# Second block of a two-block transformer: earlier norm sums, attention heads in pairs, one key chain, and low parts of weights moved from GpSimd to VectorE

## The chip, the cores and the metric

One core of one Trainium2 chip. The metric is the device time of one execution in microseconds (us). The kernel before took 2730.98 us (median of three runs, 2726.55 to 2734.91).

## The reference, cut to what matters

512 tokens, width 1024, two model blocks of two layers each, all in float32. The change touches the mixers of the second block only: the first layer adds retention (4 heads) and sliding-window attention (8 heads, 2 key/value heads), the second axial attention (8 heads, 2 key/value heads); each is followed by a feed-forward layer.

```python
def rms_norm_2(x, g):
    y = xf * lax.rsqrt(jnp.mean(xf * xf, axis=-1, keepdims=True) + EPS)
    return (y * g.astype(jnp.float32)).astype(x.dtype)
...
y = rms_norm_2(fwd + bwd, gn_gain.reshape(RET_HEADS, RET_DV))
return jax.nn.silu(g) * y
...
s = jnp.einsum('bqkgd,bjkd->bkgqj', qi, k, preferred_element_type=jnp.float32) * scale
p = jax.nn.softmax(s, axis=-1)
return jnp.einsum('bkgqj,bjkd->bqkgd', p.astype(v.dtype), v)
```

Queries and keys of both attentions pass an rms norm over the 128 numbers of a head; the window attention adds a bias and a sink to the softmax.

## The kernel before

Every product in float32 is made of three matmuls: each operand is split into a high part (`h`, `xh`) and a low part (`lo`, `xl`), and `mm3` (L413, L414, L415) adds high·high, low·high and high·low; such a group is called a triple below. Activations lie transposed, 128 of the 1024 features on the partitions and the 512 tokens along the row. `gemm` makes 128 output columns from a weight slab of 8 x 128 x 128 with 8 triples; `values` (L1031 to L1033) makes 256 columns for 128 tokens at a time with 32 triples of half the width, so it needs two slabs.

`fetch` brings each weight slab: a DMA into `w`, the high part on ScalarE (`h`, L394), the low part by a subtraction (`lo`, L395) on VectorE (DVE). For the last 24 slabs of the retention and window layer and the last 14 of the axial layer, `idle(i)` puts that subtraction on GpSimd (POOL).

A norm goes through three steps. TensorE (PE) adds the squares of a token by a product with ones (`tokens`, L481; for queries L1071). A chain of small DVE operations on 128 x 4 numbers (`rsqrt`, L492: a first guess and three Newton steps) makes the inverse root. `bcast` splits the result, multiplies it into an identity (`ssp`, two DVE operations), and PE spreads it over the partitions (L521), from where ScalarE copies it (L525).

`even` does retention by heads: query and key, two gate products, values, then the retention products; the norm of a head is finished by `head_end` in the next head's turn, with sums, chain and broadcast in one call ahead of the gates (the scheduler put the broadcast into the second gate). It then does the window attention, `attend` for one head at a time: scores (L1096 to L1098), softmax on DVE and ScalarE, transposes of the probabilities (L1125), product with the values (L1135 to L1137). Between a head's scores and its transposes comes the query product of the head after the next. `odd` does the same for axial attention, with the rotary products of a query on DVE and their sum on POOL (`rp`, L421). Keys have a chain of their own each (`kscale`).

Each engine works through its own queue in order. A scheduler writes these queues from the order of the calls and from priorities (`high_priority`). PSUM tiles have the tags `acc` (3 buffers), `s` (2), `tr` (2) and `o` (1).

Of the kernel before, what the change touches and what calls it, by code (L numbers as in the profile page):

```python
# [16 lines left out]
S = 512  # L17
# [282 lines left out]
def build(tc, a, upto=None):  # L300
# [74 lines left out]

    n_ffn = len(ffn_plan("w_mlp_up_2", "w_mlp_down_2", 1))
    odd1 = len(plan) - n_ffn
    even1 = odd1 - 20 - n_ffn
# [669 lines left out]
    def ksquare(mk, acc):  # L1048
        sq = Sum(own=mk("ksq"))
        sq.add(acc)  # L1050
        return sq

    def kscale(mk, sq, name):

        m = sq.tokens(P, 0.0)
        mul(m, m, rt[:, NB:])
        nc.vector.tensor_scalar_add(m, m, EPS)
        y = rsqrt(m)
        mul(y, y, rt[:, 0:NB])
        return bcast(y, out=mk(name))  # L1060

    def qsquare(mk, mkp, acc):
        f = mk("qsf")
        nc.scalar.activation(f, acc, AF.Square)
        return f

    def qstats(qs, i, sp):
        st_ps = ps("s")
        for b in range(NB):
            o = st_ps[:, 2 * b:2 * b + 1]  # L1070
            nc.tensor.matmul(o, sp[:, b * P:(b + 1) * P], onesf[:, 0:1], start=True, stop=True)  # L1071
        nc.vector.tensor_copy(qs[:, i], st_ps[:, 0:2 * NB].rearrange("p (b t) -> p b t", t=2)[:, :, 0])

    def qscale(qs):

        for i in range(2):
            stt(qs[:, i], qs[:, i], 1.0 / P, rt[:, NB:])
# [7 lines left out]
    def attend(mp, q, k, v, vcol, qs, bias, sink, oT, near):  # L1085
# [3 lines left out]
        lohi = [(max(0, b - 1) * P, min(NB, b + 2) * P) if near else (0, S) for b in range(NB)]  # L1089
        pt = []  # L1090
        for b in range(NB):
            lo, hi = lohi[b]
            n = hi - lo
            s = ps("s")
# [22 lines left out]
        yield  # L1117
        o = ps("o")
        order = (1, 0, 2, 3) if near else range(NB)
        for i, kb in enumerate(order):  # L1120
            b0, b1 = (max(0, kb - 1), min(NB, kb + 2)) if near else (0, NB)
            tr = ps("tr")
            for b in range(b0, b1):
                c = kb * P - lohi[b][0]
                nc.tensor.transpose(tr[:, b * P:(b + 1) * P], pt[b][:, c:c + P], ident)  # L1125
            pr = mp.tile([P, 2, S], F32R, name="pt", bufs=3)
            c0, c1 = b0 * P, b1 * P
            split(pr[:, 0, c0:c1], pr[:, 1, c0:c1], tr[:, c0:c1])
            f1 = c1
            if i == 0 and c1 < S:  # L1130
                nc.gpsimd.memset(pr[:, 0, c1:].bitcast(F32), 0.0)
                f1 = S
# [4 lines left out]
            nc.tensor.matmul(o[:, c0:c1], v1, pr[:, 0, c0:c1], start=False, stop=i == NB - 1)  # L1137
        split(oT[:, 0], oT[:, 1], o)

    def even(getr, xs, finish):  # L1140
# [6 lines left out]
        with contextlib.ExitStack() as st:  # L1147
# [5 lines left out]
            gacc = [gate(0, 0)]  # L1153
            y, later = getr()
            gacc.append(gate(0, 1))
# [5 lines left out]
            def head_end(h, sq, of, gs):  # L1161
                rr = bcast(rsqrt(sq.tokens(256)), out=mk("rr"), tag="s")
# [8 lines left out]
            for h in range(RH):  # L1171
# [42 lines left out]
                done = (h, sq, of, gs)  # L1214
            kacc = gemm2(*[slab(_gemm(e, 0, _rng(S_K + P * i))) for i in range(2)])
            head_end(*done)

        with contextlib.ExitStack() as st:
            mp = pool("sw", 1, st)
            mk = lambda name: mp.tile([P, S], F32, name=name, tag="p", bufs=NP)  # L1220
            mkp = lambda: mp.tile([P, 2, S], F32R, name="pt", bufs=3)
            ks = []
            sqk = [ksquare(mk, acc) for acc in kacc]
            vs = values(e, S_V, lambda: mp.tile([P, 2, 256], F32R, name="v", bufs=4))
            for i in range(2):
                m = kscale(mk, sqk[i], "km")
# [4 lines left out]
                ks.append(k)  # L1231

            qs, qq = {}, {}

            def query(h):

                g, i = divmod(h, 2)
                if h >= 8:
                    return
                if i == 0:  # L1240
                    qs[g] = mp.tile([P, 2, NB], F32, name="qs", bufs=3)
                acc = gemm(slab(_gemm(e, 0, _rng(S_Q + P * h))))
                q = mp.tile([P, 2, S], F32R, name="q", bufs=4)
                split(q[:, 0], q[:, 1], acc, vc("swa_q_norm_2"))
                qstats(qs[g], i, qsquare(mk, mkp, acc))
                qq[h] = q
                if i == 1:
                    qscale(qs[g])

            for h in range(2):  # L1250
                query(h)
            for h in range(SWH):
                g, i = divmod(h, 2)
                bias = mp.tile([P, 384], F32, name="bias", bufs=2)
                nc.sync.dma_start(bias, bias_view(h))
                oT = yo()
                at = attend(mp, qq[h], ks[h // 4], vs, P * (h // 4), qs[g][:, i], bias, vc("sink", h), oT, True)
                next(at)
                query(h + 2)
                list(at)  # L1260
                sw.append(oT)
                k0 = SWA_FILL[g]
                if i == 1 and k0 is not None:
                    outproj("w_out_even_2", k0, ys[k0:k0 + 4] if k0 < 8 else sw[0:4], xs)
# [4 lines left out]
    def odd(getr, xs, finish):  # L1269
# [6 lines left out]
        with contextlib.ExitStack() as st:  # L1276
            mp = pool("ax", 1, st)
            mk = lambda name: mp.tile([P, S], F32, name=name, tag="p", bufs=NP)
# [3 lines left out]
            tk = [mk("tk") for _ in range(2)]  # L1282
            for i in range(2):
                nc.vector.tensor_scalar_mul(tk[i], tab[:, i], vc("ax_k"))
            ks = []
            sqk = [ksquare(mk, acc) for acc in accs]
            fk = [rope(mk, acc, tk) for acc in accs]
            for i in range(2):
                nc.vector.tensor_scalar_mul(tab[:, i], tab[:, i], vc("ax_q"))
            vs = values(o, D + 256, lambda: mp.tile([P, 2, 256], F32R, name="v", bufs=4))  # L1290
            for i in range(2):
                m = kscale(mk, sqk[i], "km")
# [4 lines left out]
            oTs, qs, qq = [], {}, {}  # L1297

            def query(h):
                g, i = divmod(h, 2)  # L1300
                if h >= 8:
                    return
                if i == 0:
                    qs[g] = mp.tile([P, 2, NB], F32, name="qs", bufs=3)
                acc = gemm(slab(_gemm(o, 0, ax_cols(P * h))))
                f = rope(mk, acc, (tab[:, 0], tab[:, 1]))
                q = mp.tile([P, 2, S], F32R, name="q", bufs=4)
                split(q[:, 0], q[:, 1], f)
                qstats(qs[g], i, qsquare(mk, mkp, acc))
                qq[h] = q  # L1310
                if i == 1:
                    qscale(qs[g])

            for h in range(2):
                query(h)
            for h in range(8):
                g, i = divmod(h, 2)
                oT = op.tile([P, 2, S], F32R, name="yo", bufs=8)
                at = attend(mp, qq[h], ks[h // 4], vs, P * (h // 4), qs[g][:, i], None, None, oT, False)
                next(at)  # L1320
                if h >= 6:
                    outproj("w_out_odd_2", 0, oTs[0:4], xs, ns=(2 * i, 2 * i + 1))
                query(h + 2)
                list(at)
                oTs.append(oT)
# [106 lines left out]
    def getr2(sq=sq):  # L1432
        y1 = rsqrt(sq.tokens(D))
        r1 = small("tr%d" % NB)
        m = sg.tokens(D, 0.0)
        with tc.high_priority(offset=60):
            mul(r1, y1, y1)
            mul(m, m, r1)
            nc.vector.tensor_scalar_add(m, m, EPS)
            y = rsqrt(m)  # L1440
            mul(rt[:, 0:NB], y, y1)
            mul(rt[:, NB:], rt[:, 0:NB], rt[:, 0:NB])

        def later():
            r1b = bcast(y1, name="r2b")
# [104 lines left out]
```

## Time and profile before

| | us |
|---|---|
| median of three runs | 2730.98 |
| lowest, highest | 2726.55, 2734.91 |
| the profiled execution | 2728.14 |
| its span | 2726.4 |
| PE busy | 2675.7 (98%) |
| DVE busy | 2030.2 (74%) |
| ACT (ScalarE) busy | 1276.3 (47%) |
| POOL busy | 165.8 (6%) |

PE is busy nearly all the time, so what can be won is where PE waits, and what it does slowly. The mixers of the second block lie at about 1430 to 1830 us (retention, window attention) and 2190 to 2410 us (axial attention). The profile's share of busy time says little there: a wait of a few us at one place is read from the list of waits and from the timeline. The granted clock of 0.993 is a mean over the span; in short stretches it is far lower.

### The profile page before, as it was taken

How to read it: one execution, taken by the hardware profiler on the slowest of the kernel's cores; microseconds unless marked ns; L12 is line 12 of the kernel's file. 1: busy time of each engine (PE TensorE's matmuls, PEld its weight loads, DVE VectorE, ACT ScalarE, POOL GpSimd, SP SyncE). 2: the span in 40 equal slices, each digit the busy share in tenths (PEclk: the TensorE clock that was granted, in tenths of full speed). 3: DMA queues.
4: the chain of work that ended last, by engine and by line, in shares of the span. 5: the costliest groups of instructions: out<-in, count | busy, mean ns of one | idle time of the engine just before them, and what ended most of it. 6: DMA issues, size and time to landing. Idle time of an engine off the chain costs nothing.

```text
span 2726.4 us, 37828 instructions
## 1 busy us (share of the span) xinstructions
PE 2675.7 (98%) x14484; PEld 2279.0 (84%) x14484; DVE 2030.2 (74%) x3860; ACT 1276.3 (47%) x2071; POOL 165.8 (6%) x127
## 2 busy tenths in 40 slices
PE   8999999999999999999998999999999989999999
PEld 6887889999877778899987877888999877789998
DVE  8647778877775677988867656679878767798785
ACT  4437654433354674543443334565434436654442
POOL 0110000000000000000010012310000032100000
PEclk9999999999999999999999999999999999999999
DMA  4331423233434224333232221223233211123332
GB/s 162 104 112 55 140 85 124 93 97 98 136 102 157 78 74 143 105 105 101 94 107 71 86 71 61 79 73 101 96 107 109 93 62 39 55 100 101 103 107 70
DMA packets 80477, 262.83 MB, mean 96 GB/s; under 512 B 9223, under 2 KB 13063, under 8 KB 80296
## 3 DMA queue, kind: packets, MB, share of 16 engines
q1 hardware_dynamic: 80296, 260.41, 29.6%
q8 instruction: 114, 1.87, 0.3%
q14 instruction: 67, 0.55, 0.1%
HBM read 248.06 MB, written 12.32 MB: 96 GB/s over the span
## 4 chain that ended last, share of the span: by engine, by line
PE 90%; DVE 6%; ACT 1%; POOL 1%; issue 1%; DMA 0%; SPq 0%; POOLq 0%; DVEq 0%; ACTq 0%
PE ps_acc L415 18%; PE ps_acc L413 18%; PE ps_acc L414 18%; PE ps_tr L415 4%; PE ps_tr L413 4%; PE ps_tr L414 4%; PE ps_s L413 3%; PE ps_s L414 3%; PE ps_s L415 3%; PE ps_o L413 1%; PE ps_o L415 1%; PE ps_o L414 1%; PE ps_tr L956 1%; POOL rp L421 1%; PE ps_acc L1031 1%
## 5 line engine op out<-in xcount | busy, mean ns | idle before, releaser
L394 ACT ACTIVATE h<-w 128x1024 fp32r<-128x1024 f32 (+1 forms) x329 | 346.7, 1055 | 724.8 <-PE ps_acc L414 416.5
L414 PE MATMUL ps_acc<-y,h 128*128 128x512 f32 x1024 | 399.9, 391 | 0.0
L415 PE MATMUL ps_acc<-y,lo 128*128 128x512 f32 x1024 | 399.9, 390 | 0.0
L413 PE MATMUL ps_acc<-y,h 128*128 128x512 f32 x1024 | 399.8, 391 | 0.0
L395 DVE TENSOR_TENSOR lo<-w,h 128x1024 fp32r<-128x1024 f32 (+1 forms) x291 | 354.1, 1218 | 48.9 <-ACT h L394 48.2
L421 DVE TENSOR_TENSOR zg<-zg,ps_acc 128x512 f32<-128x512 f32 x304 | 207.6, 684 | 215.0 <-PE ps_acc L415 214.7
L413 PE MATMUL ps_acc<-xh,h 128*128 128x512 f32 x816 | 328.1, 402 | 0.0
L415 PE MATMUL ps_acc<-xh,lo 128*128 128x512 f32 x816 | 327.9, 402 | 0.0
L414 PE MATMUL ps_acc<-xl,h 128*128 128x512 f32 x816 | 326.4, 400 | 0.0
L415 PEld LDWEIGHTS ps_acc<-y,lo 128*128 128x128 f32 x1024 | 192.3, 188 | 40.8
L413 PEld LDWEIGHTS ps_acc<-y,h 128*128 128x128 f32 x1024 | 192.2, 188 | 37.1 <-ACT y L633 1.1
L414 PEld LDWEIGHTS ps_acc<-y,h 128*128 128x128 f32 x1024 | 192.3, 188 | 36.4 <-DVE y L634 0.8
L413 PE MATMUL ps_tr<-xh,h 128*128 128x256 f32 (+1 forms) x592 | 184.2, 311 | 8.0 <-ACT h L394 7.4
L415 PEld LDWEIGHTS ps_acc<-xh,lo 128*128 128x128 f32 x816 | 155.5, 191 | 34.7 <-issue 1.7
L413 PEld LDWEIGHTS ps_acc<-xh,h 128*128 128x128 f32 x816 | 155.5, 191 | 34.3 <-issue 2.3
L414 PEld LDWEIGHTS ps_acc<-xl,h 128*128 128x128 f32 x816 | 155.7, 191 | 33.9 <-issue 1.0
L415 PE MATMUL ps_tr<-xh,lo 128*128 128x256 f32 (+1 forms) x592 | 183.9, 311 | 0.0
L414 PE MATMUL ps_tr<-xl,h 128*128 128x256 f32 (+1 forms) x592 | 182.6, 309 | 0.0
L429 ACT ACTIVATE sh<-w 128x512 fp32r<-128x512 f32 x224 | 136.2, 622 | 59.6 <-PE ps_o L414 27.0
L430 DVE TENSOR_TENSOR sl<-w,sh 128x512 fp32r<-128x512 f32 x224 | 147.6, 682 | 0.0
L415 PE MATMUL ps_s<-th,sl 128*128 128x256 f32 x448 | 126.6, 283 | 0.0
L413 PE MATMUL ps_s<-th,sh 128*128 128x256 f32 x448 | 126.5, 282 | 0.0
(401 smaller groups left out, 6180.3 us busy)
## 6 DMA issues: line engine op xcount, KB each, us to landing
w<-w SPq DMA_DIRECT2D x439, 512.0 KB, 3.5
md<-gz SPq DMA_DIRECT2D x16, 256.0 KB, 2.5
m<-md SPq DMA_DIRECT2D x16, 256.0 KB, 3.9
x0t<-xT SPq DMA_DIRECT2D x8, 256.0 KB, 5.6
m<-xT SPq DMA_DIRECT2D x8, 256.0 KB, 4.6
xd<-zg SPq DMA_DIRECT2D x8, 256.0 KB, 2.6
m<-xd SPq DMA_DIRECT2D x8, 256.0 KB, 4.2
out<-zg SPq DMA_DIRECT2D x8, 256.0 KB, 2.0
```

What stands on the lines that cost most here:

```text
L394: nc.scalar.activation(h[:, c], w[:, c], AF.Copy)
L395: (nc.gpsimd if idle(i) else nc.vector).tensor_sub(lo[:, c], w[:, c], h[:, c].bitcast(F32))
L413: nc.tensor.matmul(out, w[0], x[0], start=first, stop=False)
L414: nc.tensor.matmul(out, w[0], x[1], start=False, stop=False)
L415: nc.tensor.matmul(out, w[1], x[0], start=False, stop=last)
L421: (eng or nc.vector).tensor_add(out, x, y)
L429: nc.scalar.activation(hi, src, AF.Copy)
L430: nc.vector.tensor_sub(lo, src, hi.bitcast(F32))
L956: nc.tensor.transpose(tr[:, b * P:(b + 1) * P], pt[b][:, kb * P:(kb + 1) * P], ident)
L1031: nc.tensor.matmul(acc, x0, wk[0], start=k == 0, stop=False)
```

## The change

- `idle` goes: all low parts of weights are made on DVE (38 subtractions move from POOL to DVE).
- The norm ahead of the first layer (`getr2`): the two inverse roots in series become one, from both sums at once. The second root, needed only for the residual, is left to `later`. Both gates of the first head come behind the sums.
- A retention head's norm: sums and chain ahead of the next head's two gates, the broadcast behind them. The last head: the values of the window attention come between.
- Keys: `kstats` makes one chain of 128 x 8 numbers for both keys, and the first query product stands between the sums and the broadcasts.
- Queries: `qstats` takes the sums of two heads from one PSUM tile straight into the chain, without a copy, at high priority.
- Attention by pairs: scores of both heads of a pair, with a query product between them, their tiles in turn under the tags `s` and `tr`; then `weigh` for each head, in which the product with the values of a block comes behind the transposes of the next.

The diff, cut to its core:

```diff
-    idle = lambda i: even1 - 24 <= i < even1 or odd1 - 14 <= i < odd1
...
-            (nc.gpsimd if idle(i) else nc.vector).tensor_sub(lo[:, c], w[:, c], h[:, c].bitcast(F32))
+            nc.vector.tensor_sub(lo[:, c], w[:, c], h[:, c].bitcast(F32))
...
+    def kstats(sps):
+        t = ps("s")
+        for i, sp in enumerate(sps):
+            sums(t, i, sp)
+        m = small("tk8", 2 * NB)
+        with tc.high_priority(offset=60):
+            for i in range(2):
+                c = slice(i * NB, (i + 1) * NB)
+                src = t[:, 2 * NB * i:2 * NB * (i + 1)].rearrange("p (b t) -> p b t", t=2)[:, :, 0]
+                stt(m[:, c], src, 1.0 / P, rt[:, NB:])
+            nc.vector.tensor_scalar_add(m, m, EPS)
+            y = rsqrt(m, 2 * NB)
+            for i in range(2):
+                mul(y[:, i * NB:(i + 1) * NB], y[:, i * NB:(i + 1) * NB], rt[:, 0:NB])
+        return [y[:, 0:NB], y[:, NB:]]
...
-            s = ps("s")
+            s = ps(("s", "tr")[b % 2])
...
+            prs.append(pr)
+            if i:
+                times(i - 1, order[i - 1])
+        times(NB - 1, order[NB - 1])
...
-            gacc = [gate(0, 0)]
             y, later = getr()
-            gacc.append(gate(0, 1))
+            gacc = [gate(0, i) for i in range(2)]
...
-            def head_end(h, sq, of, gs):
-                rr = bcast(rsqrt(sq.tokens(256)), out=mk("rr"), tag="s")
+            def head_end(y, h, of, gs):
+                rr = bcast(y, out=mk("rr"), tag="s")
...
                 if done:
-                    head_end(*done)
+                    y = rsqrt(done[0].tokens(256))
+                    last = done[1:]
...
+                if done:
+                    head_end(y, *last)
                 vs = values(e, R_V + 256 * h, lambda: mp.tile([P, 2, 256], F32R, name="rv", bufs=5))
...
-            head_end(*done)
+            y = rsqrt(done[0].tokens(256))
+            sv = values(e, S_V, lambda: op.tile([P, 2, 256], F32R, name="v", bufs=4))
+            head_end(y, *done[1:])
...
+            ys_k = kstats(sqk)
+            query(0)
             ks = []
             for i in range(2):
-                m = kscale(mk, sqk[i], "km")
+                m = bcast(ys_k[i], out=mk("km"))
...
+            for g in range(4):
+                p0 = probs(2 * g)
+                query(2 * g + 2)
+                p1 = probs(2 * g + 1)
+                if g == 3:
+                    outproj("w_out_odd_2", 0, oTs[0:4], xs, ns=(0, 1))
+                mix(2 * g, p0)
+                query(2 * g + 3)
+                scale(g + 1)
...
+                mix(2 * g + 1, p1)
...
-        y1 = rsqrt(sq.tokens(D))
+        m1 = sq.tokens(D)
...
-            mul(r1, y1, y1)
-            mul(m, m, r1)
-            nc.vector.tensor_scalar_add(m, m, EPS)
+            stt(m, m1, EPS, m, op1=ALU.add)
```

Three places of the engines' queues, before and after. Line numbers after the change are 6 smaller around these places (L407 to L409 are the triple, L515 is the broadcast's matmul, L389 the low part, L412, L418 and L424 the product, the scaled product and the split).

PE, fourth retention head: `ps_s` is the broadcast of the third head's norm, `ps_acc` a gate product or, with 256 columns, the values. Before:

```order
L415 MATMUL ps_acc_14771<-xh_87,lo_14453 128x512
L413 MATMUL ps_acc_14805<-xh_87,h_14643 128x512
L414 MATMUL ps_acc_14805<-xl_88,h_14643 128x512
L415 MATMUL ps_acc_14805<-xh_87,lo_14644 128x512
L413 MATMUL ps_acc_14805<-xh_87,h_14643 128x512
L414 MATMUL ps_acc_14805<-xl_88,h_14643 128x512
L521 MATMUL ps_s_14751<-ssp_14746,ones_83 128x512
L415 MATMUL ps_acc_14805<-xh_87,lo_14644 128x512
L521 MATMUL ps_s_14751<-ssp_14746,ones_83 128x512
```

Now:

```order
L408 MATMUL ps_acc_14780<-xl_88,h_14640 128x512
L409 MATMUL ps_acc_14780<-xh_87,lo_14641 128x512
L515 MATMUL ps_s_14816<-ssp_14811,ones_83 128x512 x2
L1025 MATMUL ps_acc_14842<-h_14680,xh_87 128x256
L1026 MATMUL ps_acc_14842<-lo_14681,xh_87 128x256
```

The broadcast stood in the second triple of the second gate, and now stands behind its last.

PE, first queries of the axial attention: `ps_o` is the broadcast of a key's norm, `ps_acc` a query product. Before:

```order
L413 MATMUL ps_acc_20990<-xh_87,h_20671 128x512
L414 MATMUL ps_acc_20990<-xl_88,h_20671 128x512
L415 MATMUL ps_acc_20990<-xh_87,lo_20672 128x512
L413 MATMUL ps_acc_20990<-xh_87,h_20671 128x512
L414 MATMUL ps_acc_20990<-xl_88,h_20671 128x512
L521 MATMUL ps_o_20935<-ssp_20930,ones_83 128x512
L415 MATMUL ps_acc_20990<-xh_87,lo_20672 128x512
```

Now:

```order
L407 MATMUL ps_acc_20904<-xh_87,h_20637 128x512
L408 MATMUL ps_acc_20904<-xl_88,h_20637 128x512
L409 MATMUL ps_acc_20904<-xh_87,lo_20638 128x512
L515 MATMUL ps_o_20948<-ssp_20943,ones_83 128x512 x2
L407 MATMUL ps_acc_20978<-xh_87,h_20746 128x512
```

The broadcast stood in the third triple of the first query product; now that whole product is ahead of it, and the second query product behind.

DVE, axial attention, the chain of the first two queries' norms (`tt8`, `ty8`) now:

```order
L1116 TENSOR_REDUCE mx_21043<-ps_tr_21075 128x1
L412 TENSOR_TENSOR tt8_21029<-ty8_21028 128x8
L389 TENSOR_TENSOR lo_21087<-w_21085,h_21086 128x1024
L418 SCALAR_TENSOR_TENSOR tt8_21029<-tt8_21029,qs_21014 128x8
L418 SCALAR_TENSOR_TENSOR ty8_21028<-tt8_21029,ty8_21028 128x8
L412 TENSOR_TENSOR tt8_21029<-ty8_21028 128x8
L418 SCALAR_TENSOR_TENSOR tt8_21029<-tt8_21029,qs_21014 128x8
L389 TENSOR_TENSOR lo_21219<-w_21217,h_21218 128x1024
L418 SCALAR_TENSOR_TENSOR ty8_21028<-tt8_21029,ty8_21028 128x8
```

Two low parts of weights, which were on POOL, now stand inside the chain on DVE.

## Rows read from the trace of the kernel before

**Rows 1.** The page's chain by engine, whole span, and its row of low parts.

```profile
PE 90%; DVE 6%; ACT 1%; POOL 1%; issue 1%; DMA 0%; SPq 0%; POOLq 0%; DVEq 0%; ACTq 0%
...
L395 DVE TENSOR_TENSOR lo<-w,h 128x1024 fp32r<-128x1024 f32 (+1 forms) x291 | 354.1, 1218 | 48.9 <-ACT h L394 48.2
```

**Rows 2.** PE's waits, 1430 to 1830: total us, times, longest.

```profile
PE ps_s L521 <- DVE ssp L418: 8.8, 4, 4.0
PE ps_acc L1031 <- DVE gs L418: 7.1, 1, 7.1
PE ps_o L521 <- DVE ssp L418: 2.9, 3, 1.9
PE ps_o L1136 <- DVE pt L430: 2.3, 3, 1.1
PE ps_tr L1125 <- DVE pt L430: 1.6, 1, 1.6
PE ps_acc L1031 <- DVE v L424: 0.7, 1, 0.7
```

**Rows 3.** The same view, 2190 to 2410 (axial attention).

```profile
PE ps_s L1096 <- ACT p L1113: 6.9, 3, 2.9
PE ps_o L521 <- DVE ssp L418: 4.2, 1, 4.2
PE ps_o L1135 <- ACT pt L429: 0.9, 1, 0.9
```

**Rows 4.** Windows: length, busy us of PE, PEld, DVE, ACT, POOL; granted clock, DMA, GB/s.

```profile
1455.00:1460.00 5.00, 4.23 (x22) 4.23 (x23) 3.65 (x7) 3.06 (x4) 1.27 (x1) 0.57 0.00 0
1495.00:1500.00 5.00, 4.04 (x11) 2.96 (x12) 4.78 (x9) 0.72 (x2) 0.00 (x0) 0.68 0.25 62
...
1630.00:1660.00 30.00, 23.87 (x120) 20.87 (x121) 22.44 (x67) 10.78 (x18) 5.53 (x4) 0.83 0.24 73
2210.00:2215.00 5.00, 4.43 (x13) 3.58 (x14) 3.25 (x7) 0.60 (x1) 0.00 (x0) 0.66 0.34 105
```

**Rows 5.** Timeline of DVE behind the first norm: start, us, engine, line, operation.

```profile
1446.30 0.68 DVE L418 TENSOR_TENSOR ssp<-ident,bl 128x512 fp32r<-128x512 f32 x1
1446.90 1.22 DVE L395 TENSOR_TENSOR lo<-w,h 128x1024 fp32r<-128x1024 f32 x1
...
1455.03 1.29 DVE L418 TENSOR_TENSOR gs<-ps_acc,rb 128x512 f32<-128x512 f32 x2
```

**Rows 6.** Timeline of PE and DVE, norm of the third retention head.

```profile
1579.64 0.48 PE L413 MATMUL ps_acc<-xh,h 128*128 128x512 f32 x1
...
1586.00 0.39 PE L413 MATMUL ps_acc<-xh,h 128*128 128x512 f32 x1
...
1588.01 0.50 PE L521 MATMUL ps_s<-ssp,ones 128*128 128x512 f32 x1 [1.38 <-DVE ssp L418]
...
1587.87 0.68 DVE L418 TENSOR_TENSOR ssp<-ident,bl 128x512 fp32r<-128x512 f32 x1
```

**Rows 7.** Timeline of DVE, norm of the last retention head.

```profile
1626.00 1.63 DVE L499 TENSOR_SCALAR ti<-tm 128x4 int32<-128x4 int32 x1
1627.67 2.42 DVE L500 TENSOR_SCALAR ty<-ti 128x4 int32<-128x4 int32 x1
```

**Rows 8.** Groups of POOL, 1425 to 2410: busy us, mean ns, idle before.

```profile
L395 POOL TENSOR_TENSOR lo<-w,h 128x1024 fp32r<-128x1024 f32 x38 | 91.2, 2401 | 255.6 <-ACT h L394 240.8 <-ACT p L1115 7.9 <-issue 4.9
L421 POOL TENSOR_TENSOR rp<-rp,rp 128x512 f32<-128x512 f32 x18 | 29.1, 1619 | 549.1 <-DVE rp L418 549.1
```

**Rows 9.** Groups of DVE, 1630 to 1830.

```profile
L424 DVE SCALAR_TENSOR_TENSOR qs<-qs,rt 128x4 f32<-128x4 f32 x8 | 10.9, 1360 | 0.2
...
L424 DVE SCALAR_TENSOR_TENSOR qs<-ty,rt 128x4 f32<-128x4 f32 x8 | 0.9, 155 | 0.1
```

**Rows 10.** Timeline of DVE, the two key norms of the axial attention.

```profile
2204.39 2.45 DVE L424 SCALAR_TENSOR_TENSOR tt<-tt,tm 128x4 f32<-128x4 f32 x2
2206.80 2.33 DVE L424 SCALAR_TENSOR_TENSOR ty<-tt,ty 128x4 f32<-128x4 f32 x2
```

**Rows 11.** Window of 100 us in the axial heads, columns as in rows 4.

```profile
2240.00:2340.00 100.00, 94.32 (x463) 72.44 (x461) 73.46 (x185) 64.37 (x124) 24.22 (x13) 1.00 0.13 37
```

More of the change, by code (lines that the diff above doesn't have):

```diff
@@ L1046, in rope, with sums, square, qstats @@
         return t1
[L1048 to L1056, printed above, removed]
[L1057 to L1063 removed]
+    def sums(t, i, sp):
+        for b in range(NB):
+            o = t[:, 2 * (NB * i + b):2 * (NB * i + b) + 1]
+            nc.tensor.matmul(o, sp[:, b * P:(b + 1) * P], onesf[:, 0:1], start=True, stop=True)
+    def kstats(sps):
[13 more added lines that the diff above has]
+        return [y[:, 0:NB], y[:, NB:]]
+    def square(f, acc):
         nc.scalar.activation(f, acc, AF.Square)
         return f
[L1067 to L1072, printed above, removed]
+    def qstats(qs, sps):
+        t = ps("s")
+        for i, sp in enumerate(sps):
+            sums(t, i, sp)
+        with tc.high_priority(offset=60):
+            for i in range(2):
+                src = t[:, 2 * NB * i:2 * NB * (i + 1)].rearrange("p (b t) -> p b t", t=2)[:, :, 0]
+                stt(qs[:, i], src, 1.0 / P, rt[:, NB:])
+            qscale(qs)
     def qscale(qs):
[L1076 to L1077 removed]
         q2 = qs.rearrange("p h b -> p (h b)")
@@ L1116, in attend, with weigh, times @@
             pt.append(p)
-        yield
+        return pt
+    def weigh(mp, pt, v, vcol, oT, near):
+        order = (1, 0, 2, 3) if near else range(NB)
         o = ps("o")
-        order = (1, 0, 2, 3) if near else range(NB)
-        for i, kb in enumerate(order):
+        prs = []
+        def times(i, kb):
             b0, b1 = (max(0, kb - 1), min(NB, kb + 2)) if near else (0, NB)
[L1122 to L1126, printed above, removed]
-            c0, c1 = b0 * P, b1 * P
[L1128 to L1132, printed above, removed]
+            c0, c1 = b0 * P, b1 * P
+            pr = prs[i]
+            f1 = S if i == 0 else c1
             vv = v[kb]
@@ L1137, in attend @@
             nc.tensor.matmul(o[:, c0:c1], v1, pr[:, 0, c0:c1], start=False, stop=i == NB - 1)
+        for i, kb in enumerate(order):
+            b0, b1 = (max(0, kb - 1), min(NB, kb + 2)) if near else (0, NB)
+            tr = ps("tr")
+            for b in range(b0, b1):
+                c = kb * P - span(near, b)[0]
+                nc.tensor.transpose(tr[:, b * P:(b + 1) * P], pt[b][:, c:c + P], ident)
+            pr = mp.tile([P, 2, S], F32R, name="pt", bufs=3)
+            c0, c1 = b0 * P, b1 * P
+            split(pr[:, 0, c0:c1], pr[:, 1, c0:c1], tr[:, c0:c1])
+            if i == 0 and c1 < S:
+                nc.gpsimd.memset(pr[:, 0, c1:].bitcast(F32), 0.0)
+            prs.append(pr)
+            if i:
+                times(i - 1, order[i - 1])
+        times(NB - 1, order[NB - 1])
         split(oT[:, 0], oT[:, 1], o)
@@ L1296, in odd, with mix @@
                 ks.append(k)
[L1297 to L1317, printed above, removed]
-                oT = op.tile([P, 2, S], F32R, name="yo", bufs=8)
[L1319 to L1324, printed above, removed]
-                oTs.append(oT)
+            query(1)
+            scale(0)
+            probs = lambda h: scores(mp, qq[h], ks[h // 4], qs[h // 2][:, h % 2], None, None, False)
+            def mix(h, pt):
+                oT = op.tile([P, 2, S], F32R, name="yo", bufs=8)
+                weigh(mp, pt, vs, P * (h // 4), oT, False)
+                oTs.append(oT)
+            for g in range(4):
+                p0 = probs(2 * g)
+                query(2 * g + 2)
+                p1 = probs(2 * g + 1)
+                if g == 3:
+                    outproj("w_out_odd_2", 0, oTs[0:4], xs, ns=(0, 1))
+                mix(2 * g, p0)
+                query(2 * g + 3)
+                scale(g + 1)
+                if g == 3:
+                    outproj("w_out_odd_2", 0, oTs[0:4], xs, ns=(2, 3))
+                mix(2 * g + 1, p1)
         open_up()
```

105 lines of the change are left out of this document (60 added, 45 removed).

## The prediction

> **What bounds the kernel.** I read the page first: PE is 98% busy and the chain that ended last is 90% PE, with DVE second at 6% [rows 1]. So time comes only from two places: stretches in which PE waits, and stretches in which it runs slowly. Next the list of PE's waits in the two stretches that the change touches. In the retention and window layer they come to some 23 us, of which 8.8 + 2.9 us are waits for `ssp`, the last DVE step before a norm's broadcast, and 7.1 us is one wait for the first gate [rows 2]. In the axial layer 6.9 us are waits for a free score tile (PE waits for ScalarE's exponential) and 4.2 us for one key broadcast [rows 3]. The rest of the 2726 us is not touched. Then the windows: behind several of these waits the granted clock falls, to 0.57, 0.68, 0.83 over 30 us, and 0.66 [rows 4]. A wait thus costs twice, once idle and once in matmuls at the lower of the two levels (1.2 against 2.4 GHz). What a dip costs I work out as PE's busy time in the window times what the clock lacks to 1. Last the timeline around each wait, to see what is late.
>
> **The change part by part.** PE does the same matmuls before and after, and the weight slabs are used and fetched in the same order, so I count only waits.
>
> *First norm.* The two chains in series become one, and the gates come behind the sums, so the broadcast is ready about a chain earlier, some 2.6 us (an estimate: 13 steps of 0.16 us [rows 9] are 2.1, and there are gaps between them). But the long wait is for `gs`, the product that frees the first gate's PSUM tile. Between `ssp` at 1446.3 and `gs` at 1455.0 DVE's queue holds a low part, the table products and the rotary products [rows 5], and all of these stay. One more pair of `ssp` for the deferred root moves ahead of them, 2 x 0.68 us. I take 1.2 us of the 7.1; bounds 0 and 7.1. The dip behind it stays.
>
> *Retention heads 1 to 3.* The third head shows the pattern: the gate begins at 1579.64, its tenth triple at 1586.00, so a triple takes 0.70 us and two gates 16 x 0.70 = 11.2 us. The last `ssp` ends at 1588.55, 8.9 us after the gate's start, and PE had waited 1.38 us at the broadcast [rows 6]. With the broadcast behind both gates the chain fits, with 2.3 us to spare, which is almost two low parts (1.22 us each). The three waits are 8.8 - 4.0 = 4.8 us [rows 2], all gone. Of the dips I count the one at 1495: 4.04 x 0.32 = 1.3 us [rows 4]. Sum 6.1; bounds 3 (one head late again) and 6.5.
>
> *Last head and the keys.* The wait of 4.0 us has a cause of its own: two steps of 128 x 4 numbers took 1.63 and 2.42 us [rows 7] where such a step takes 0.16 [rows 9], at the time of POOL's first low parts. With the values (32 triples, 11 us) between sums and broadcast, and with no low part on POOL, both causes go. The key chain is one instead of two and has a query product of 8 x 0.70 = 5.6 us as cover. Waits of 4.0 + 0.7 + 2.5 us (the 2.9 less 0.4 for the first norm) lie here [rows 2]; I take 6.8 of 7.2. The dip over 1630 to 1660 costs 23.87 x 0.17 = 4.1 us [rows 4]; I take 3.5. Sum 10.3; bounds 6 and 11.3.
>
> *Window attention.* 2.3 + 1.6 us of waits for `pt` [rows 2]. Transposing a block ahead of the preceding block's product hides the split of `pt`; but the scores now hold `tr` tiles too, so a transpose can wait for an exponential. I take half, 2.0; bounds -3 and 3.9.
>
> *Axial keys.* Two pairs of steps of the chains took 2.45 and 2.33 us [rows 10], where a pair at 0.16 each is 0.3 at most; without them, and with the whole first query product ahead of the broadcast, the 4.2 us go, and the dip: 4.43 x 0.34 = 1.5 us. Sum 5.7; bounds 4.2 and 5.7.
>
> *Axial heads.* 6.9 + 0.9 us [rows 3]. Four score tiles instead of two take the first wait away, but the pairs bring two softmaxes onto DVE and ScalarE at once. I leave 3 us: gain 4.8; bounds -5 and 7.8.
>
> *Low parts on DVE.* 38 subtractions leave POOL, at 2.40 us each [rows 8], and cost DVE 1.22 us each [rows 1], 46 us. On the other side, DVE's small steps no longer stretch: `qs` took 1.36 us, eight times, where 0.155 is usual, 9.7 us [rows 9], and rows 7 and 10 hold 3.7 + 4.2 us more. So DVE gains at most 46 - 18 = 28 us of work over 620 us. In the axial heads it is 73.5% busy [rows 11]; POOL ran 13 instructions there, seven of them low parts, and 7 x 1.22 us make that 82, under PE's 94. I cost it at nothing while that cover stands; where a chain is awaited, one low part ahead costs 1.2 us, and two now stand inside the chain of the first axial queries. Bounds 0 and 12 lost.
>
> A rule speaks against this part. What the rows show is that DVE's small steps are held up while POOL subtracts [rows 7, 9]. The Trainium skill (GPSIMD Engine Reference, Key points) says that GpSimd shares its SBUF interfaces with VectorE and contends with instructions that have two SBUF inputs. The moved subtractions have two SBUF inputs, so by that page each could now hold up one of the 18 rotary sums left on POOL. It is the third rival.
>
> Sum: 1.2 + 6.1 + 10.3 + 2.0 + 5.7 + 4.8 = 30.1 us. The profiled execution took 2728.1, so 2698.0; it lay 2.9 us under the median of 2731.0, and half of that added gives **2699 us**.
>
> **The rivals.** *DVE becomes the bound in the attentions* (22%). The norms' waits go, but DVE's extra work and two softmaxes at once bring waits in the attention heads: the gains there (6.8) are lost, and 10 us of new waits come. For it: DVE's 82% in an in-order queue, and the low parts inside a chain [rows 11]. Against: PE waited for DVE there only for `pt`, not for the queue at large [rows 2, 3]. Time 2699 + 17 = 2716.
>
> *The waits move* (8%). The chains end earlier, but PE stalls at what is late next, the exponentials or the `tr` tiles, by as much. It gives 2723 to 2739, no change that can be measured. Against it: some 16 us of the gain lie in norm waits with more than 2 us to spare.
>
> *The rotary sums are late* (5%). A low part on DVE falls on each of the ten sums in the axial layer and delays it by its own 1.22 us, and the query's scores with it: 12 us at most, 2711. Against: POOL sat idle 549 us for work from DVE [rows 8], so the sums themselves are not the bottleneck.
>
> *Slower: low parts ahead of awaited chains* (5%). POOL waited 240.8 us for ScalarE's high parts [rows 8], at no cost to others. On DVE such a wait stops the whole queue, softmax included. If each of the 38 stops an awaited chain for its 1.22 us and 0.7 us of waiting, 73 us come back, and the kernel takes 2772. It decides against the change from 40 us, that is 1.05 us per low part on the path. Against: the 291 low parts already on DVE let it idle 48.2 us in all, 0.17 each [rows 1].
>
> **How the numbers follow.** The forecast itself has 60%, with a range of 2686 (nearly all waits and the dips gone) to 2711. To keep 8 in 10, the range reaches into the first rival: **2686 to 2719**. A measurement of this kernel can tell about 0.3% (8 us) from no change. Faster by more needs a time under 2723: the forecast, the rotary rival and nearly all of the first rival, 0.86; within 0.3%: 0.08; slower: 0.06.
>
> **What would show it.** In the profile after: no waits for `ssp` at the heads' broadcasts and at the keys (16 us); the wait for `gs` still at 5 to 6 us with its dip; clock 1.0 from 1490 to 1660 and at the axial keys; the low parts on DVE at 1.22 us and no small step over 1 us; 2 to 6 us of waits left in the axial heads. I am wrong if waits for `p`, `pt` or `mx` in the attentions exceed 12 us, if DVE's wait for the high parts grows by 20 us or more, or if the dips stay without the waits.

## The result, and the profile after

The changed kernel takes 2683.3 us (median of four runs, 2681.33 to 2685.68) against 2728.8 before (median of four, one more than above): ratio 0.9831, 95% interval 0.9810 to 0.9853. It is 45.5 us faster. The forecast of 2699 had the direction and most of the places right and the size wrong: the time lies 2.7 us under the range (2686 to 2719).

The profiled execution has a span of 2683.0 us in place of 2726.4, so 43.4 us less. PE's work between two layers gives it by parts. The last product of a feed-forward layer and the sums of squares (`ssq`) ahead of the next one enclose a layer's mixer. Timeline of PE (start, us, engine, line, operation), before:

```profile
1420.20 0.39 PE L415 MATMUL ps_acc<-y,lo 128*128 128x512 f32 x1
...
1849.53 0.95 PE L481 MATMUL ps_s<-onesf,ssq 128*128 128x1 f32 x8
...
2189.27 0.95 PE L481 MATMUL ps_s<-onesf,ssq 128*128 128x1 f32 x8
...
2393.12 0.95 PE L481 MATMUL ps_s<-onesf,ssq 128*128 128x1 f32 x8
```

The same four places after:

```profile
1420.71 0.39 PE L409 MATMUL ps_acc<-y,lo 128*128 128x512 f32 x1
...
1824.84 0.95 PE L475 MATMUL ps_s<-onesf,ssq 128*128 128x1 f32 x8
...
2164.42 0.94 PE L475 MATMUL ps_s<-onesf,ssq 128*128 128x1 f32 x8
...
2350.69 0.94 PE L475 MATMUL ps_s<-onesf,ssq 128*128 128x1 f32 x8
```

The first layer's mixer went from 429.3 to 404.1 us (25.2 less), the feed-forward layer between stayed at 339.7 and 339.6, the axial part went from 203.8 to 186.3 (17.6 less, unrounded). PE's waits after, over the whole span (us in total, times, longest):

```profile
PE ps_tr L407 <- ACT h L388: 7.4, 1, 7.4
PE ps_acc L1025 <- DVE gs L412: 6.3, 1, 6.3
PE ps_acc L1025 <- DVE v L418: 0.9, 1, 0.9
PE ps_acc L407 <- DVE zg L415: 0.8, 1, 0.8
PE ps_o L1138 <- ACT pt L423: 0.6, 1, 0.6
PE ps_o L515 <- DVE ssp L412: 0.5, 2, 0.3
PE ps_tr L1147 <- DVE p L418: 0.4, 1, 0.4
```

The first row is the start of the program, as before. Of all that stood in [rows 2, 3] only the wait for `gs` is left (7.1 then), and less than 4 us of small ones. The windows after, columns as in [rows 4]:

```profile
1450.00:1455.00 5.00, 0.00 (x0) 0.00 (x0) 4.22 (x8) 0.63 (x1) 1.86 (x2) 0.59 0.10 41
1455.00:1460.00 5.00, 4.96 (x23) 4.96 (x24) 2.27 (x4) 3.07 (x4) 0.68 (x1) 0.50 0.00 0
1460.00:1465.00 5.00, 5.00 (x39) 5.00 (x39) 0.97 (x2) 0.95 (x2) 0.00 (x0) 0.88 0.01 3
1490.00:1500.00 10.00, 10.00 (x49) 8.32 (x48) 8.38 (x18) 3.92 (x6) 2.24 (x1) 1.00 0.34 106
1620.00:1650.00 30.00, 30.00 (x182) 26.25 (x182) 22.94 (x58) 13.11 (x21) 0.00 (x0) 1.00 0.39 119
2170.00:2190.00 20.00, 19.11 (x113) 17.31 (x113) 15.76 (x45) 5.71 (x9) 2.84 (x2) 0.91 0.26 79
...
2200.00:2300.00 100.00, 99.39 (x499) 80.03 (x498) 80.10 (x216) 69.58 (x135) 10.75 (x7) 1.00 0.16 48
```

From 1490 to 1500 and from 1620 to 1650 the clock is 1.00 now. At 2170 to 2190, ahead of the axial keys, it is 0.91. In the axial heads PE is busy 99.4 of 100 us in place of 94.3 [rows 11], and DVE 80.1 in place of 73.5, as foretold (82). The dip behind the `gs` wait is still there, at 0.50, and not smaller than before.

DVE's small steps, groups of 1620 to 1800 (busy us, mean ns, idle before):

```profile
L389 DVE TENSOR_TENSOR lo<-w,h 128x1024 fp32r<-128x1024 f32 x24 | 29.2, 1222 | 4.6 <-ACT h L388 4.2 <-PE ps_acc L409 0.4
...
L418 DVE SCALAR_TENSOR_TENSOR qs<-ps_s,rt 128x4 f32<-128x4 f32 x8 | 0.9, 156 | 4.6 <-PE ps_s L1046 4.6
```

The step on `qs` that took 1360 ns [rows 9] takes 156, but it is no longer the same step: it now reads the sums from PSUM and no longer a copy in SBUF, the memory of all tiles that are not in PSUM. Which of the two changes made it short is read from the experiments. One sign failed: five steps of 128 x 4 or 128 x 8 numbers in the second block still take 1.23 to 1.26 us (18 took over 1 us before), each while a rotary sum runs on GpSimd. Of the whole program, the page's row of low parts and its line of engines:

```profile
L389 DVE TENSOR_TENSOR lo<-w,h 128x1024 fp32r<-128x1024 f32 (+1 forms) x329 | 400.5, 1218 | 51.2 <-ACT h L388 49.1
...
PE 2661.4 (99%) x14484; PEld 2275.8 (85%) x14484; DVE 2028.0 (76%) x3852; ACT 1274.4 (47%) x2071; POOL 78.7 (3%) x89
```

DVE took over 38 x 1.22 = 46 us of low parts and is busy 2028.0 us, where it was 2030.2.

### The profile page after: what moved, and what is told of

Same layout as the page of the kernel before. It is cut to its first block, busy times and chain, and to the rows that moved or that the text cites. A ratio compares the mean times of both kernels' runs of the same rounds, so it can differ in the third digit from the quotient of the medians.

```text
span 2683.0 us, 37767 instructions
## 1 busy us (share of the span) xinstructions
PE 2661.4 (99%) x14484; PEld 2275.8 (85%) x14484; DVE 2028.0 (76%) x3852; ACT 1274.4 (47%) x2071; POOL 78.7 (3%) x89
## 4 chain that ended last, share of the span: by engine, by line
PE 96%; DVE 3%; ACT 0%; issue 0%; DMA 0%; SPq 0%; POOL 0%; DVEq 0%; ACTq 0%; POOLq 0%
PE ps_acc L407 20%; PE ps_acc L409 19%; PE ps_acc L408 19%; PE ps_tr L409 4%; PE ps_tr L407 4%; PE ps_tr L408 4%; PE ps_s L407 3%; PE ps_s L408 3%; PE ps_s L409 3%; PE ps_o L407 1%; PE ps_o L409 1%; PE ps_o L408 1%; PE ps_acc L1025 1%; PE ps_tr L1147 1%; PE ps_acc L1027 1%; PE ps_acc L1026 1%
## 5 line engine op out<-in xcount | busy, mean ns | idle before, releaser
L389 DVE TENSOR_TENSOR lo<-w,h 128x1024 fp32r<-128x1024 f32 (+1 forms) x329 | 400.5, 1218 | 51.2 <-ACT h L388 49.1
L407 PE MATMUL ps_acc<-y,h 128*128 128x512 f32 x1024 | 399.9, 391 | 0.0
L409 PE MATMUL ps_acc<-y,lo 128*128 128x512 f32 x1024 | 399.9, 391 | 0.0
L407 PE MATMUL ps_acc<-xh,h 128*128 128x512 f32 x816 | 326.6, 400 | 0.0
L409 PE MATMUL ps_acc<-xh,lo 128*128 128x512 f32 x816 | 325.1, 398 | 0.0
L409 PEld LDWEIGHTS ps_acc<-y,lo 128*128 128x128 f32 x1024 | 192.2, 188 | 40.8
L407 PEld LDWEIGHTS ps_acc<-y,h 128*128 128x128 f32 x1024 | 192.3, 188 | 37.1 <-ACT y L627 1.1
L407 PE MATMUL ps_tr<-xh,h 128*128 128x256 f32 (+1 forms) x592 | 184.0, 311 | 7.4 <-ACT h L388 7.4
L409 PE MATMUL ps_tr<-xh,lo 128*128 128x256 f32 (+1 forms) x592 | 183.7, 311 | 0.1
L409 PEld LDWEIGHTS ps_acc<-xh,lo 128*128 128x128 f32 x816 | 154.3, 189 | 34.7 <-issue 1.4
L407 PEld LDWEIGHTS ps_acc<-xh,h 128*128 128x128 f32 x816 | 154.5, 189 | 34.3 <-issue 2.3
L424 DVE TENSOR_TENSOR sl<-w,sh 128x512 fp32r<-128x512 f32 x224 | 147.5, 681 | 0.0
L409 PE MATMUL ps_s<-th,sl 128*128 128x256 f32 x448 | 126.6, 283 | 0.0
L407 PE MATMUL ps_s<-th,sh 128*128 128x256 f32 x448 | 126.5, 282 | 0.0
```

Of the source, the lines that this page charges most:

```text
L389: nc.vector.tensor_sub(lo[:, c], w[:, c], h[:, c].bitcast(F32))
L407: nc.tensor.matmul(out, w[0], x[0], start=first, stop=False)
L409: nc.tensor.matmul(out, w[1], x[0], start=False, stop=last)
L424: nc.vector.tensor_sub(lo, src, hi.bitcast(F32))
```

## The experiments

Lengths of the two mixers (first layer, axial) are read as above, from the profiled execution; for comparison 429.3 and 203.8 before, 404.1 and 186.3 after the change. Ratios are to the kernel before, runs of the same session. Its median was 2728.8 us in the session of the change, 2729.0 in that of the next four runs, 2729.9 in that of the next three and 2731.7 in that of the last three (query sums as before, both edits together, the best of both), so differences of medians across sessions are uncertain by up to 3 us.

**Low parts back on GpSimd.** The change with one line undone (and the definition of `idle` back, not shown):

```diff
-            nc.vector.tensor_sub(lo[:, c], w[:, c], h[:, c].bitcast(F32))
+            (nc.gpsimd if idle(i) else nc.vector).tensor_sub(lo[:, c], w[:, c], h[:, c].bitcast(F32))
```

> The changed kernel with the 38 low parts put back on GpSimd, all orders as changed. Theory (the orders give cover to the norms, and GpSimd's low parts only stretch DVE's small steps, which the cover partly hides): 8 to 20 us slower than the change, 2691 to 2703, with DVE's small steps at 1 to 2.5 us again. Rival 1 (GpSimd's low parts were the main cause of the old waits): 30 us or more slower, 2713 and above. Rival 2 (only the order matters): within 4 us of 2683.

2698.4 us, ratio 0.9886 (0.9871 to 0.9901), so 15 us slower than the change, with 3.7 us in the first layer and 9.5 in the axial one. The time is the theory's. With GpSimd's subtractions PE waits again at scores for a tile that an exponential still holds (L1106 is the first matmul of a score, L1123 the exponential: 2.0 + 0.8 us), and at one transpose (L1152) for `pt`. Behind the waits for the first weights and for `gs` (6.8 and 6.3 us) the rows are:

```profile
PE ps_tr L1106 <- ACT p L1123: 2.0, 2, 1.2
PE ps_tr L1152 <- DVE pt L429: 1.3, 1, 1.3
PE ps_o L520 <- DVE ssp L417: 1.3, 4, 0.6
PE ps_s L1051 <- ACT ksq L1071: 1.2, 1, 1.2
PE ps_s L1106 <- ACT k L428: 1.0, 1, 1.0
PE ps_o L1143 <- ACT pt L428: 1.0, 1, 1.0
...
PE ps_s L1106 <- ACT p L1123: 0.8, 1, 0.8
```

DVE is busy 2012.6 us here and 2028.0 in the change, so 46.3 us of moved work cost it 15.4: in this order the stretching is 31 us. One thing is not as expected. The orders were to be those of the change, but the scheduler plans anew: in the two mixers some 440 of 3037 matmuls stand elsewhere in PE's queue, by a comparison of the two traces. The 15 us are those of the edit with its new plan.

**Only that line changed in the kernel before.**

```diff
-            (nc.gpsimd if idle(i) else nc.vector).tensor_sub(lo[:, c], w[:, c], h[:, c].bitcast(F32))
+            nc.vector.tensor_sub(lo[:, c], w[:, c], h[:, c].bitcast(F32))
```

> The kernel before with this one edit: all low parts on DVE, no order changed. Theory: the waits that were made by stretched steps go (last head 2 to 3 us, keys 2 us, axial keys 4 us) with their dips (5 us), the others stay: 2711 to 2720. Rival 1 (GpSimd was the main cause): 2700 or below. Rival 2 (DVE gets too full, or nothing hangs on it): 2725 and above.

2709.5 us, ratio 0.9927 (0.9912 to 0.9942): 19.5 us faster than the before of its session, a little more than the theory gave, and 9.5 us from the first rival's bound. The page's line shows what the 46 us cost DVE:

```profile
PE 2669.6 (99%) x14484; PEld 2278.9 (84%) x14484; DVE 2036.3 (75%) x3898; ACT 1277.2 (47%) x2071; POOL 76.3 (3%) x89
```

DVE's busy time grew by 6.1 us (2030.2 to 2036.3) for 46.3 us more work. So 91 us of subtraction on GpSimd [rows 8] had stretched DVE's instructions by 40 us. The trace of the kernel before shows it instruction by instruction. In the second block (from 1400 us on) 114 DVE instructions overlap a low part on GpSimd, and they took 35.6 us longer than the medians of their forms in the change; the 1746 that overlap nothing on GpSimd took 0.8 us longer in all. Of the eight `qs` steps, six overlap a low part, and each of these ends within 0.02 us of the low part's end: the step is held until GpSimd's subtraction is over. Here, with the step unchanged and the low parts on DVE, it takes 159 ns:

```profile
L424 DVE SCALAR_TENSOR_TENSOR qs<-qs,rt 128x4 f32<-128x4 f32 x8 | 1.3, 159 | 0.1
```

The change's own form of the step needs no such help. In the run with the low parts back on GpSimd (above) four of the eight overlap one, in that with single heads and GpSimd (below) all eight, and all took 0.15 to 0.16 us: with one operand in PSUM the step is not held. Waits of PE, first rows behind that for the first weights:

```profile
PE ps_acc L1031 <- DVE gs L418: 7.1, 1, 7.1
PE ps_s L521 <- DVE ssp L418: 5.1, 4, 2.1
PE ps_tr L1125 <- ACT p L1115: 3.9, 3, 2.0
PE ps_s L1071 <- ACT qsf L1064: 2.6, 2, 2.0
PE ps_s L481 <- ACT ksq L470: 2.2, 1, 2.2
```

Of the wait of 4.0 us at the last head's broadcast 0.3 is left and that of 4.2 at the axial key is gone, without any call being moved; the three of the other heads stay (4.8 us). But here too the scheduler planned anew (some 490 of 3037 matmuls stand elsewhere). It put 43 matmuls of 0.12 us between the last head's sums and its broadcast, where there were 26, and 18 of the first axial query product ahead of the key's broadcast, where there were 8. From the first sum to the first broadcast the two norms now take 6.4 and 10.0 us in place of 8.1 and 11.9. So of the two waits 1.7 and 1.9 us went by a faster chain, and about 2.0 and 2.3 by the queue's new order. The new waits for squares (`ksq`, `qsf`) and `p` are the other side of it.

**A head's norm as before.**

```diff
                 if done:
-                    y = rsqrt(done[0].tokens(256))
-                    last = done[1:]
+                    head_end(rsqrt(done[0].tokens(256)), *done[1:])
...
-                if done:
-                    head_end(y, *last)
...
-            sv = values(e, S_V, lambda: op.tile([P, 2, 256], F32R, name="v", bufs=4))
             head_end(y, *done[1:])
+            sv = values(e, S_V, lambda: op.tile([P, 2, 256], F32R, name="v", bufs=4))
```

> The changed kernel with a retention head's norm as before: sums, chain and broadcast together ahead of the gates, and for the last head ahead of the window values. Theory: three waits of 1 to 2 us, one of 2 to 3 for the last head and the dips behind them come back: 8 to 14 us slower, 2691 to 2697. Rival (without GpSimd's low parts the chains are fast enough): within 3 us of 2683.

2689.7 us, ratio 0.9855 (0.9840 to 0.9869): 6.4 us slower, 5.4 of it in the first layer. It is less than I expected (8 to 14), because the last head hardly waits (0.3 us). What came back is

```profile
PE ps_s L515 <- DVE ssp L412: 4.5, 4, 1.4
```

three waits of 1.4 us and a fourth of 0.3.

**One head at a time.**

```diff
-            s = ps(("s", "tr")[b % 2])
+            s = ps("s")
...
-            if i:
-                times(i - 1, order[i - 1])
-        times(NB - 1, order[NB - 1])
+            times(i, kb)
...
+            for h in range(8):
+                g, i = divmod(h, 2)
+                p0 = probs(h)
+                if h >= 6:
+                    outproj("w_out_odd_2", 0, oTs[0:4], xs, ns=(2 * i, 2 * i + 1))
+                query(h + 2)
+                if i == 1:
+                    scale(g + 1)
+                mix(h, p0)
```

The window attention is changed in the same way.

> The changed kernel with both attentions one head at a time: scores under the tag s alone, next query, then transposes each followed by its own product; chains and low parts as changed. Theory: PE waits again for score tiles and for the split of pt, 8 to 12 us, 2691 to 2696. Rival (those waits came from a DVE held up by GpSimd): within 3 us of 2683.

2686.3 us, ratio 0.9843 (0.9826 to 0.9859): 3.0 us slower, so the rival. The axial layer is 3.6 us longer, the first layer 2.1 us shorter. The pairs help in one layer and hurt in the other. The sizes are blurred by the clock: this profile has no dip at 2178, which costs the change 1.7 us, so in the axial layer the pairs are worth about 5; and of the 2.1 us in the first layer 0.7 are a shorter dip behind the `gs` wait, the rest two waits (0.8 us for `zg`, 0.4 for `p`).

**First query product behind the key broadcasts.**

```diff
             ys_k = kstats(sqk)
-            query(0)
             ks = []
...
+            query(0)
             query(1)
```

> The changed kernel with the first query product behind the key broadcasts in both layers; one chain for both keys stays. Theory (the query product is the cover of the key chain): waits of 2 to 3 us at each of the two places and a dip behind each, 5 to 9 us slower, 2688 to 2692. Rival (the scheduler fills the place with other products, or the chain alone is fast enough): within 2 us of 2683.

2684.7 us, ratio 0.9833 (0.9817 to 0.9850), both layers as in the change (403.8 and 186.4). The time is the rival's, and the trace tells why: the scheduler put the query product back. In the axial layer 17 matmuls of the first query product stand ahead of the first key broadcast (24 in the change, 8 in the kernel before), in the first layer 19, as in the change. So the edit hardly took the cover away, and whether the key chain needs it stays open.

**Query sums as before**, each behind its square, with a copy and without the higher priority:

```diff
-    def qstats(qs, sps):
-        t = ps("s")
-        for i, sp in enumerate(sps):
-            sums(t, i, sp)
...
+    def qstats(qs, i, sp):
+        st_ps = ps("s")
...
+        nc.vector.tensor_copy(qs[:, i], st_ps[:, 0:2 * NB].rearrange("p (b t) -> p b t", t=2)[:, :, 0])
```

> The changed kernel with the queries' norm sums as before: sums right behind each query's square, a copy out of PSUM, a chain per pair without the higher priority for its ends; pairs, key chain, low parts and norms as changed. Theory (a good part of what no run has yet found lies here, since the kernel before with low parts on DVE waits 2.6 us for a query's squares and 3.9 us for late probabilities in the axial layer): 4 to 8 us slower, 2687 to 2691. Rival (the chains are not awaited): within 2 us of 2683.

2689.2 us, ratio 0.9846 (0.9831 to 0.9861): 5.9 us slower by the medians (4.1 by the two ratios), as the theory said. The axial layer has 4.4 of it (1.7 of that in one more dip), and the new wait is that of the sums (L1073) for a tile `s` that the exponential still holds:

```profile
PE ps_s L1073 <- ACT p L1117: 2.6, 2, 1.3
```

**One head at a time and low parts on GpSimd**, both edits together.

> The changed kernel with both attentions one head at a time and with the 38 low parts on GpSimd. Theory (the axial waits for a free score tile come from DVE's steps stretched by GpSimd, and the pairs are the lesser part): slower than single heads alone by 12 to 20 us, 2698 to 2706, and the waits for ScalarE's exponential come back as a group. Rival (the pairs are what hides the softmax, GpSimd only delays norms): 3 to 8 us slower than single heads alone.

2707.9 us, ratio 0.9913 (0.9898 to 0.9927): 21.6 us slower than single heads alone, a little over the theory's range (19 by the two ratios, inside it). But the kind of wait is another: not mainly the exponential, as I had written, but `pt` and `ssp`:

```profile
PE ps_o L1144 <- DVE pt L429: 4.8, 7, 1.2
PE ps_o L520 <- DVE ssp L417: 2.3, 4, 1.2
```

**Gate products first.** The two products that free the gates' PSUM tiles ahead of the rotary table on DVE:

```diff
+            gs0 = []
+            for i in range(2):
+                f = mk("gs")
+                mul(f, gacc[i], rb)
+                nc.scalar.activation(f, f, AF.Silu)
+                gs0.append(f)
             for i in range(2):
                 mul(tab[:, i], tab[:, i], rb)
```

> The changed kernel with the first head's two gate products with rb moved ahead of the rotary table and the rotary products in DVE's queue. Theory (the 6.3 us wait is DVE's order alone, and the dip behind it goes with it): 8 to 11 us faster than the change, 2672 to 2675. Rival (what is late next, the rotary products or the values' splits, takes the place of the wait): 0 to 4 us faster.

2677.8 us, ratio 0.9813 (0.9798 to 0.9827): 5.5 us faster than the change, between theory and rival. The first layer is 7.4 us shorter (396.7). The wait is not gone but turned into a shorter one for the values' split:

```profile
PE ps_acc L1025 <- DVE rv L418: 1.6, 1, 1.6
```

So 4.7 us came from the wait, and 2.7 from the dip that is no longer there.

**Idle products in the wait**, 27 matmuls that nobody reads:

```diff
+                if h == 0:
+                    for j in range(9):
+                        t = ps("s")
+                        mm3(t, (xh[:, 0, 0:P], xl[:, 0, 0:P]), (xh[:, 1], xl[:, 1]), True, True)
                 vs = values(e, R_V + 256 * h, lambda: mp.tile([P, 2, 256], F32R, name="rv", bufs=5))
```

> The changed kernel with 27 matmuls of 128x512 on data that nobody reads put into PE's queue behind the first broadcast, where PE waits 6.3 us for the gate; the result is the same. Theory (the granted clock falls because PE is idle there, and the matmuls behind run at half speed for some us): 2 to 4 us faster although PE does 6.3 us more work, and no dip at 1450 to 1465. Rival (what follows is bound by DVE in any case, or the clock does not depend on this wait): 0 to 2 us slower.

2681.3 us, ratio 0.9825 (0.9811 to 0.9840): 2 us faster than the change by the medians, which the intervals do not part. The profile is clearer: the first layer is 2.5 us shorter (401.6), with the clock at 1.00 where the change has 0.59 and 0.50:

```profile
1450.00:1455.00 5.00, 4.62 (x38) 4.38 (x37) 3.45 (x6) 1.49 (x3) 1.85 (x2) 1.00 0.00 0
1455.00:1460.00 5.00, 5.00 (x45) 5.00 (x44) 2.00 (x5) 3.41 (x6) 0.00 (x0) 1.00 0.01 3
```

Busy time by lacking clock gives 4.96 x 0.50 + 5.00 x 0.12 = 3.1 us for the dip of the change, so that way of pricing a dip is about right.

**The best of both**: gate products first, single heads in the window attention alone, pairs in the axial one.

```diff
-            s = ps(("s", "tr")[b % 2])
+            s = ps("s" if near else ("s", "tr")[b % 2])
...
+            if near:
+                times(i, kb)
+            elif i:
+                times(i - 1, order[i - 1])
```

> The version with the gate products first, and in it the window attention one head at a time (scores under the tag s, products right behind their transposes) while the axial attention stays in pairs. Theory (the two edits act in different layers and add up: 6.4 us from the gate, 1.9 us from the single window heads, as the first layer measured by itself in the two runs): 1 to 3 us faster than gate first alone, 2674 to 2677. Rival (the 1.9 us were the luck of one execution): within 1 us of 2678.

2675.9 us, ratio 0.9795 (0.9779 to 0.9812), the fastest kernel here: 2.0 us under gate first alone by the medians, and its first layer 1.5 us shorter (395.2). It beats the change by 7.4 us by the medians (across sessions; 9.8 by the two ratios). The step from gate first is in the direction of the theory, and no larger than the intervals can tell; its 1.5 us are mostly the waits for `zg` and `p`, which are gone here too.

## Why the prediction was wrong

Of the 43.4 us between the two profiled spans 29.0 were PE's waits (16.4 in the first layer, 12.0 in the axial one, 0.6 behind it, summed from the timeline); the other 14.4 lie in PE's busy time. The prediction had 23.8 and 6.3, so 5.2 and 8.1 us are missing from its sum.

- *First norm*, 1.2 us: right for the waits. 7.1 + 0.4 became 6.3, for the reason given: `gs` stands behind the rotary products on DVE, and the run with the gate products first showed that it is the order (one matmul moved in PE's queue, 4.7 of 6.3 us gone). The dip behind it cost 9.23 x 0.21 = 1.9 us before (1455 to 1465) and 3.1 in this execution, which takes the gain back.
- *Retention heads*, 6.1 us: right. The waits are gone, and undoing the order alone costs 6.4 us.
- *Last head and keys*, 10.3 us: the size was right (all 7.2 us of waits and the dip are gone), and both causes are seen: with the low parts moved and no call, about half of the 4.0 us goes by a faster chain and half by more matmuls ahead of the broadcast. What the query product in front of the key broadcasts is worth was not shown.
- *Axial keys*, 5.7 us: right in size and place. With the low parts alone the 4.2 us go too, again half by each cause. But PE's unchanged wait of 0.9 us ahead of it now has a dip of its own (0.91 over 2170 to 2190, 19.11 x 0.09 = 1.7 us), which gives some of it back.
- *Axial heads*, 4.8 us, and *window attention*, 2.0: too small. I left 3 and 1.9 us of waits for transposes behind exponentials and a fuller DVE, of which 0.6 and 1.2 came; and I counted no dip, though one at 2235 to 2245 cost 8.59 us busy x 0.17 = 1.5. The rows called the waits a matter of score tiles and exponentials, and I credited the pairs with them. But without pairs the 6.9 us for score tiles [rows 3] are 1.4 once DVE has the low parts, and undoing the pairs costs 3.0 us in all.
- *Low parts on DVE*: a first step that failed. I summed the stretched steps of three groups to 18 us, subtracted that from 46, put the 28 us of new DVE work at nothing, gave the range 12 us for its harm, and left 4.9 us of waits in the attentions. But the stretching was 40 us in the old order and 31 in the new one, so DVE got 6 or 15 us of new work, and of those waits 1.8 us came. The move alone (with the plan that the scheduler makes of it) made the kernel before 19.5 us faster, and undone in the change it costs 15. It was the largest single part. The prediction counted it as a gain only in the last head's chain and the axial keys, where I had seen the long steps; in its own term it stood as a risk.
- *"So I count only waits"*: the second step that failed, by size the larger. It has no term for a matmul that starts late while PE counts as busy. The record of a matmul of 512 columns lasts 0.39 us, but the next usually starts 0.23 us behind it (rows below), so a start up to 0.16 us late is in no list of waits. Counted from the start times of both traces, outside the dips, 207 matmuls of the two mixers before and 145 after start more than 0.025 us later than is usual behind their form. Their lateness sums to 21.1 and 13.2 us: 7.9 us that the sum put at nothing. The same count in the undone runs gives back 1.4 us (low parts), 1.9 (a head's norm) and 1.5 (pairs). What makes these starts late stays open: for most of them the profile shows no wait.

Timeline of PE before, axial heads at a clock of 1.00. The distances of the starts are 0.23, 0.32 and 0.34 us, and no idle time is shown:

```profile
2339.56 0.40 PE L414 MATMUL ps_acc<-yo,h 128*128 128x512 f32 x1
2339.79 0.40 PE L415 MATMUL ps_acc<-yo,lo 128*128 128x512 f32 x1
2340.11 0.50 PE L1096 MATMUL ps_s<-k,q 128*128 128x512 f32 x1
2340.45 0.39 PE L1097 MATMUL ps_s<-k,q 128*128 128x512 f32 x1
```

The runs also settle the rivals. DVE did not become the bound. What the Trainium skill (GPSIMD Engine Reference, Key points) states of the shared SBUF interfaces is that GpSimd contends with DVE instructions that have two SBUF inputs or run in a 2-port perf mode. The trace agrees for two inputs, on both sides. The `qs` step was held with two inputs in SBUF (1360 ns, 159 without the subtractions) and not with one. And the 18 rotary sums left on GpSimd did get slower, from 1619 [rows 8] to 1808 ns, as the third rival had it: one that overlaps a low part on DVE takes 2.2 to 2.4 us (nine of them, six before), of the others eight take 1.3 and one 1.7. Whether the stretched steps with one input [rows 7] ran in such a mode no run shows.

```profile
L415 POOL TENSOR_TENSOR rp<-rp,rp 128x512 f32<-128x512 f32 x18 | 32.5, 1808 | 615.7 <-DVE rp L412 577.2 <-ACT p L1118 21.7 <-ACT pt L423 12.6
```

PE waits for none of them. Low parts did not stop DVE either: its idle time before them went from 48.9 [rows 1] to 51.2 us with 38 more of them. Nor did the waits move: the waits for `p` and `pt` in the attentions are 1.0 us.

Two things stay open: the sum of the parts and the share of the plan. The undone parts do not add up to the whole: 15.1 + 6.4 + 3.0 + 5.9 + 1.4 and 1.2 for the first norm are 33 of 45.5 us. Some of the rest is interplay, since single heads and GpSimd's low parts together cost 24.6 us (22 by the ratios) where they cost 18.1 one by one; the single key chain was not undone by itself. And the scheduler's new plan stands beside the stretching as a cause of what the moved low parts are worth: no run has the low parts moved and every queue else as it was.

The 14.4 us in PE's busy time come out nearly. The dips give 1.3 + 4.1 + 1.5 + 1.5 us by the windows named, less 1.7 and 1.2 that the change has more in others, 5.5 in all (6.8 counted from the start times); the late starts give 7.9, so 13.4 to 14.7 together.

## What to carry to other kernels

Work put on an idle GpSimd is not free when DVE works beside it: compare DVE's total busy time with and without it, not only the rows that look odd, before calling it cover. A PE that is 98% busy can still hide 20 us of late starts, so compare start times, not only waits. When PE is the bound, splitting the call of a chain of small DVE steps hides it: sums early, broadcast behind the next product (6.4 us here). When a scheduler writes the queues, look in the trace at whether an edit changed the order that it was meant to change, and no other. And look at what a freed PSUM tile waits for in its releaser's queue: moving two products ahead of others there was worth 5.5 us, the merged chain and the earlier sums ahead of them 1.2.

## What the hardware showed that I had not expected

- 38 subtractions of 2.40 us on GpSimd lengthened DVE's own instructions by 40 us of busy time in the old order and by 31 in the new one, 0.44 and 0.34 us for each us of GpSimd's work. A step of 128 x 4 numbers with two inputs in SBUF ended with GpSimd's subtraction (up to 2.2 us); with one of them in PSUM it took 0.16 beside it.
- Waiting was dearer than useless work: with 27 unread matmuls in a wait of 6.3 us the layer took 2.5 us less; the granted clock stayed at 1.00.
- The same wait of 0.9 us for `v` in the axial layer was followed by 0.91 over 20 us in the change's profile, and by no dip in that of the idle products, where it lies at 2171.6:

```profile
2170.00:2180.00 10.00, 9.12 (x59) 8.20 (x59) 8.94 (x34) 3.69 (x6) 0.50 (x1) 1.00 0.36 109
2180.00:2190.00 10.00, 9.95 (x47) 7.87 (x46) 8.32 (x12) 5.74 (x9) 1.75 (x1) 1.00 0.23 59
```

A dip behind a short wait is thus worth one or two us either way from one execution to the next, and a term for it in a sum should be a range.
